# The first layer's mixer shift, scale and gate on TensorE alone, and the first tile turned while their matrices land

## The chip, the cores and the metric

The kernel runs on one core of one Trainium2 chip. The metric is device time in microseconds (us) of one execution; the median of several is compared. Its engines are named as the profile names them: PE (TensorE), DVE (VectorE), ACT (ScalarE), POOL (GpSimd) and SP (SyncE), which issues the DMAs.

## The reference

One inference step of a trunk of two layers, 256 context tokens and 1,024 latent tokens, 1,024 wide. Each sub-layer normalises its rows, applies a scale and a shift that come from a condition vector, runs a mixer or a feed-forward block, and adds the result under a gate from the same condition. What the change touches is the condition's part:

```python
def modulation(cond, w_mod, b_mod):
    m = jax.nn.silu(cond) @ w_mod + b_mod
    return jnp.split(m[:, None, :], 6, axis=-1)

def sublayer_in(x, g, shift, scale):
    return rms_norm(x, g) * (1 + scale) + shift

def sublayer_out(x, y, g, gate):
    return x + gate * rms_norm(y, g)
...
    sh_p, sc_p, gt_p, fsh_p, fsc_p, fgt_p = modulation(c_ctx[None, :], mod_w[l], mod_b[l])
    sh_s, sc_s, gt_s, fsh_s, fsc_s, fgt_s = modulation(c, mod_w[l], mod_b[l])
    hp = sublayer_in(xp, norm_mix_pre[l], sh_p, sc_p)
```

There are two conditions (one for context, one for latents), and `mod_w[l]` is 1,024 x 6,144 in f32: six parts of 1,024 x 1,024. Part 0 is the mixer's shift, part 1 its scale, part 2 its gate.

## The kernel before, in words

Tokens are worked on in ten tiles of 128 rows, in the order 2 to 9, 0, 1 (`ORDER`). A part of `mod_w` is read as eight k tiles of 128 x 1,024 (512 KB each). There are three ways of multiplying a k tile with the two conditions. On DVE, `total[c] = r * cond[k, c] + total[c]` for both c, and at the end four matmuls with `pick` sum the 128 partitions on PE. Or on PE alone: `cond32[:, k]`, the condition padded with zeros to 32 columns, is the stationary operand, and the k tile streams past it in two matmuls of 512 columns. `mod_steps` before mixes both for parts 0 and 1 (`SHARED`: the odd k tiles go to PE, the even ones to DVE, and the pick matmuls add DVE's sums to PE's); the gate (`gate_steps`, part 2) uses DVE and pick, in halves of 512 columns.

**The opening.** Parts 0 and 1 are computed first, from eight buffers `wt`. The result, 64 rows with the two halves at rows 0 and 32, is turned by four small transposes and put into `mods`. Meanwhile the first tile of x is loaded and normalised (`front_rows`), the K/V weights (two units) are loaded and split into a high and a low part (ACT casts, POOL or DVE subtracts), and so are the four Q units.

**The front.** For each tile, a list of events (`weave`, numbers in units of a step; event e of the i-th tile is at i + e) sets by hand the order on PE, DVE, ACT and POOL: `front_load` (x), `front_square` (ACT), `front_rstd` (DVE and POOL), `front_hat` (DVE scales the rows), `front_turn` (PE: eight transposes into an A bank pair), `front_mod` (ACT: eight pieces with `mods`), `front_hi` (DVE: high part into `hh`), `front_lo` (POOL: low part into `hl`), `front_kv` (PE: 24 matmuls of 256 columns), `front_q` (PE: 24 of 512), then head norms, rotary turns (`head_scale`, L489; `head_sum`, L508), the transposed keys and queries and their stores. The gate's generator is advanced twice per tile (0.5 and 0.95). After the front the attention of the latents starts.

SP's order isn't written by hand. It issues one DMA after the other, each waiting for its buffer. Buffers that matter: `wt` 8, `raw` 3 (x tiles, the gate's matrices, the cache), PSUM `bank` B 3, `bank2` A 2.

Of the kernel before, what the change touches and what calls it, by code (L numbers as in the profile page):

```python
# [31 lines left out]
SHARED = (1, 3, 5, 7)  # L32
# [17 lines left out]
def trunk_kernel(ctx: ExitStack, tc: tile.TileContext, A: dict, O: dict):  # L50
# [168 lines left out]
    def mod_steps(l, part, make=None, shared=()):  # L219


        total = [s5([P, D]) for _ in range(2)]

        def load(k):
            r = (make or raw)([P, D])
            SP.dma_start(r, A["mod_w"][l, rows(k), part * D : (part + 1) * D])
            return r

        if shared:
            acc = [bank((64, 512)) for _ in range(2)]  # L230
        nxt = load(0)
        yield
        for k in range(KT):
            r, nxt = nxt, load(k + 1) if k < KT - 1 else None
            if k == 5:
                res = t2([64, 512])
                SP.dma_start(res, A["mod_b"][l, part])
            if k in shared:
                for j in range(2):
                    PE.matmul(acc[j][32 * j : 32 * j + 32, :], cond32[:, k], r[:, 512 * j : 512 * j + 512], start=k == min(shared), stop=False)  # L240
                continue
            for c in range(2):
                if k == 0:
                    DVE.tensor_scalar(total[c], r, cond[:, k, c : c + 1], None, op0=ALU.mult)
                else:
                    DVE.scalar_tensor_tensor(total[c], r, cond[:, k, c : c + 1], total[c], op0=ALU.mult, op1=ALU.add)  # L246
                if c == 0 and (l, part) > (0, 4):
                    yield
            yield
# [5 lines left out]
        if shared:  # L255
            for j in range(2):
                h = slice(32 * j, 32 * j + 32)
                DVE.tensor_tensor(res[h], acc[j][h], res[h], op=ALU.add)
        else:
            DVE.tensor_tensor(res, acc[0][0:64], res, op=ALU.add)  # L260
        yield
        w, what = part // 3, part % 3
        if what == 2:
            for j in range(2):
                SP.dma_start(gate_d[l, w, :, j * 512 : j * 512 + 512], res[32 * j : 32 * j + 2, :])
            return
# [4 lines left out]
        for r in range(2):  # L271
            src = tv[:, :, :, r].rearrange("p b j -> p j b")
            dst = mods[:, l, w, r, 1 - what, :].rearrange("p (j b) -> p j b", b=4)
            if what == 0:
                DVE.tensor_copy(dst, src)
            else:
                gg = gpre[:, l, w, :].rearrange("p (j b) -> p j b", b=4)
                DVE.scalar_tensor_tensor(dst, src, 1.0, gg, op0=ALU.add, op1=ALU.mult)
        yield
# [167 lines left out]
    with tc.manual_schedule(engines=every):  # L447
        finish(mod_steps(0, 0, wt, SHARED))
        front_load(ORDER[0])
        kv_raw = [s5([P, 1024]) for _ in range(2)]  # L450
        for i in range(2):
            SP.dma_start(kv_raw[i], A["wall"][U_KV + i])
        steps = mod_steps(0, 1, wt, SHARED)
        for _ in range(3):
            next(steps)
        front_rows(ORDER[0])
# [4 lines left out]
        finish(steps)  # L461
    early_tiles = ORDER[:1]
# [76 lines left out]
    def front_turn(t):  # L539
        st["tr", t] = tr = bank2((P, KT, P))  # L540
# [109 lines left out]
    def gate_steps(l, w):  # L650

        for j in range(2):
            c = slice(512 * j, 512 * j + 512)
            total = [t2([P, 512]) for _ in range(2)]
            for k in range(KT):
                r = raw([P, 512])
                SP.dma_start(r, A["mod_w"][l, rows(k), (3 * w + 2) * D + 512 * j : (3 * w + 2) * D + 512 * j + 512])
                yield
                for c in range(2):
                    if k == 0:  # L660
                        DVE.tensor_scalar(total[c], r, cond[:, k, c : c + 1], None, op0=ALU.mult)
                    else:
# [5 lines left out]
            yield  # L668
            DVE.tensor_tensor(bias, acc, bias, op=ALU.add)
            SP.dma_start(gate_d[l, w, :, 512 * j : 512 * j + 512], bias[0:2])  # L670
# [3 lines left out]
        (0.06, front_load), (0.5, lambda t: next(front_part, None)), (0.857, front_square), (0.95, front_rstd),  # L674
# [1030 lines left out]
```

## Time and profile before

| | |
|---|---|
| median of 3 runs | 3441.93 us (3436.46 to 3443.43) |
| profiled execution, own time | 3447.16 us |
| its span | 3445.4 us |
| PE busy | 3265.6 us (95%) |
| DVE busy | 2094.1 us (61%) |
| ACT busy | 1266.3 us (37%) |
| POOL busy | 1179.4 us (34%) |
| granted PE clock, mean | 0.982 |

Busy shares are averages over stages with different limits. The granted clock is told as a share: 1.00 is 2.4 GHz, 0.50 is 1.2 GHz, and what lies between is a stretch with some of both.

### The profile page before, as it was taken

The numbers are of one execution on the slowest core, as the hardware profiler recorded it, in microseconds if no ns is written. First come the engines' busy times: TensorE is split into PE (matmuls) and PEld (weight loads), VectorE is DVE, ScalarE is ACT, GpSimd is POOL, SyncE is SP. The second block draws the span as 40 slices with busy tenths as digits, with TensorE's granted clock in tenths as the row PEclk, the third lists the DMA queues.
The fourth block names the chain that finished last, engine by engine and source line by source line (L and its number), as shares of the span: only waits on it lengthen the run. The fifth ranks groups of instructions, "written<-read, shape, count | busy, mean of one in ns | idle before, by whom it ended". The sixth has DMA issues, their size and how long they took to land. (4 is left out here: it accounts for less than half of the span.)

```text
span 3445.4 us, 44445 instructions
## 1 busy us (share of the span) xinstructions
PE 3265.6 (95%) x17258; PEld 2723.2 (79%) x17258; DVE 2094.1 (61%) x3589; ACT 1266.3 (37%) x2529; POOL 1179.4 (34%) x742
## 2 busy tenths in 40 slices
PE   5789999999999999999899999999999999999998
PEld 3667777888878878888778888887778888888886
DVE  7879988546666664344866666666574444344347
ACT  3467863451111111112566666656531111111113
POOL 3556667451111111113644433335221111111134
PEclk8889999999999999999999999999999999999999
DMA  5210023442222221112411111113431111111124
GB/s 208 69 37 14 19 89 114 155 145 87 87 87 88 88 84 40 38 37 86 177 58 45 47 47 45 49 65 97 126 116 45 39 42 43 37 37 37 38 91 165
DMA packets 106211, 260.03 MB, mean 75 GB/s; under 512 B 10240, under 2 KB 45952, under 8 KB 106000
## 3 DMA queue, kind: packets, MB, share of 16 engines
q1 hardware_dynamic: 106000, 257.20, 22.5%
q8 instruction: 135, 2.21, 0.3%
q14 instruction: 76, 0.62, 0.1%
HBM read 221.34 MB, written 35.82 MB: 75 GB/s over the span
## 5 line engine op out<-in xcount | busy, mean ns | idle before, releaser
L1097 DVE TENSOR_TENSOR s<-s,B 128x512 f32<-128x512 f32 x840 | 559.9, 685 | 565.2 <-PE B L192 564.5
L176 POOL TENSOR_TENSOR w<-raw,w 128x1024 fp32r<-128x1024 f32 x163 | 402.6, 2472 | 1408.0 <-ACT w L175 1403.8
L190 PE MATMUL A<-hh,w 128*128 128x512 f32 (+1 forms) x2112 | 755.0, 357 | 3.5 <-DVE s L330 2.2
L192 PE MATMUL A<-hh,w 128*128 128x512 f32 (+1 forms) x2112 | 750.3, 355 | 2.8 <-POOL w L176 2.8
L191 PE MATMUL A<-hl,w 128*128 128x512 f32 (+1 forms) x2112 | 747.7, 354 | 0.0
L190 PEld LDWEIGHTS A<-hh,w 128*128 128x128 f32 x2112 | 397.5, 188 | 69.5 <-issue 5.9
L192 PEld LDWEIGHTS A<-hh,w 128*128 128x128 f32 x2112 | 397.2, 188 | 66.0 <-POOL w L176 4.0
L191 PEld LDWEIGHTS A<-hl,w 128*128 128x128 f32 x2112 | 397.4, 188 | 62.8
L175 ACT CAST w<-raw 128x1024 fp32r<-128x1024 f32 x166 | 174.2, 1049 | 712.7 <-PE B L191 416.1
L190 PE MATMUL B<-w,s 128*128 128x512 f32 x880 | 351.2, 399 | 14.2 <-DVE s L1097 13.5
L192 PE MATMUL B<-w,s 128*128 128x512 f32 x880 | 348.2, 396 | 9.7 <-DVE s L176 8.7
L191 PE MATMUL B<-w,s 128*128 128x512 f32 x880 | 344.0, 391 | 0.0
L1078 ACT ACTIVATE t<-A,c 128x512 f32<-128x512 f32 (+1 forms) x132 | 81.2, 615 | 703.2 <-PE A L192 703.2
L374 PE MATMUL B<-c,s 128*128 128x128 f32 x1344 | 205.8, 279 | 46.8 <-DVE w L390 23.4
L374 PEld LDWEIGHTS B<-c,s 128*128 128x128 f32 x1344 | 155.8, 141 | 90.6 <-DVE w L390 35.7
L190 PE MATMUL C<-hh,w 128*128 128x512 f32 (+1 forms) x576 | 213.0, 370 | 5.2 <-ACT s L1200 1.8
L390 DVE TENSOR_TENSOR t<-B,t 128x512 fp32r<-128x512 f32 (+2 forms) x216 | 127.6, 591 | 142.9 <-ACT t L384 129.6
L190 PEld LDWEIGHTS B<-w,s 128*128 128x128 f32 x880 | 165.3, 188 | 59.2 <-DVE s L1097 27.0
L1079 DVE TENSOR_TENSOR t<-t,A 128x512 f32<-128x512 f32 (+1 forms) x132 | 78.9, 598 | 218.6 <-ACT t L1078 218.6
L192 PEld LDWEIGHTS B<-w,s 128*128 128x128 f32 x880 | 165.4, 188 | 52.5 <-DVE s L176 12.7
L192 PE MATMUL C<-hh,w 128*128 128x512 f32 (+1 forms) x576 | 205.4, 357 | 0.0
L191 PE MATMUL C<-hl,w 128*128 128x512 f32 (+1 forms) x576 | 205.3, 356 | 0.0
(283 smaller groups left out, 6178.9 us busy)
## 6 DMA issues: line engine op xcount, KB each, us to landing
raw<-wall SPq DMA_DIRECT2D x171, 512.0 KB, 3.3
raw<-mod_w SPq DMA_DIRECT2D x72, 512.0 KB, 3.9
x_d<-s SPq DMA_DIRECT2D x30, 512.0 KB, 2.6
w<-wall SPq DMA_DIRECT2D x22, 512.0 KB
raw<-x SPq DMA_DIRECT2D x20, 512.0 KB, 3.9
s<-x_d SPq DMA_DIRECT2D x20, 512.0 KB
s<-wall SPq DMA_DIRECT2D x17, 512.0 KB, 3.4
w<-mod_w SPq DMA_DIRECT2D x16, 512.0 KB, 9.3
```

The lines of the kernel that those rows point to most:

```text
L175: ACT.copy(hi, src)
L176: (eng or DVE).tensor_tensor(lo, src, f32(hi), op=ALU.subtract)
L190: PE.matmul(out, sh, mh, start=i == 0, stop=False)
L191: PE.matmul(out, sh, ml, start=False, stop=False)
L192: PE.matmul(out, sl, mh, start=False, stop=i == n - 1)
L374: PE.transpose(tr[:, at : at + P], self.p[a][:, col : col + P], ident)
L390: DVE.tensor_tensor(tl[:, 0:n], tr[:, 0:n], f32(th[:, 0:n]), op=ALU.subtract)
L1078: ACT.activation(s, acc[:, 0, 0:n], AF.Silu, bias=zerob)
L1079: DVE.tensor_tensor(s, s, acc[:, 1, 0:n], op=ALU.mult)
L1097: DVE.tensor_tensor(yt, yt, part, op=ALU.add)
```

## The change

Parts 0 and 1 come from PE alone. The matrices of both are loaded in one row (the first eight into the eight `wt` buffers, each of part 1 as soon as the matmuls of the same k of part 0 are through), and each is multiplied by two matmuls when it is there; the two halves go to different 32-row groups of PSUM. x of the first tile is loaded ahead of everything, normalised at once and turned on PE between the third and fourth matrix of part 1. The gate of the first layer's mixer is multiplied on PE too, one k tile per step with the full 1,024 columns, into 32 rows of an A bank pair that it holds through the front. x of the second tile is loaded ahead of the Q units. `mod_steps` loses its shared form; for the other parts it stays as it was.

```diff
@@ -216,54 +215,13 @@
-    def mod_steps(l, part, make=None, shared=()):
...
-        if shared:
-            acc = [bank((64, 512)) for _ in range(2)]
...
-            if k in shared:
-                for j in range(2):
-                    PE.matmul(acc[j][32 * j : 32 * j + 32, :], cond32[:, k], r[:, 512 * j : 512 * j + 512], start=k == min(shared), stop=False)
-                continue
-            for c in range(2):
-                if k == 0:
-                    DVE.tensor_scalar(total[c], r, cond[:, k, c : c + 1], None, op0=ALU.mult)
-                else:
-                    DVE.scalar_tensor_tensor(total[c], r, cond[:, k, c : c + 1], total[c], op0=ALU.mult, op1=ALU.add)
-                if c == 0 and (l, part) > (0, 4):
-                    yield
...
-        if not shared:
-            acc = [bank_c()] * 2
-        for j in range(2):
-            for c in range(2):
-                PE.matmul(acc[j][32 * j : 32 * j + 32, :], pick[:, c, :], total[c][:, 512 * j : 512 * j + 512], start=c == 0 and not shared, stop=c == 1)
...
+    def mod_load(l, part, k, make):
+        r = make([P, D])
+        SP.dma_start(r, A["mod_w"][l, rows(k), part * D : (part + 1) * D])
+        return r
+
+    def mod_put(l, w, what, res):
+
         tr = bank_c((P, 4, 64))
         for b in range(4):
             PE.transpose(tr[:, b, :], res[:, b * P : (b + 1) * P], ident[0:64, 0:64])
...
+    def first_mods():
+
+        parts = [(part, k) for part in range(2) for k in range(KT)]
+        there = {item: mod_load(0, *item, wt) for item in parts[:KT]}
+        acc, res = {}, {}
+        for part, k in parts:
+            if k == 0:
+                acc[part] = [bank((64, 512)) for _ in range(2)]
+                res[part] = t2([64, 512])
+                SP.dma_start(res[part], A["mod_b"][0, part])
+            r = there.pop((part, k))
+            for j in range(2):
+                PE.matmul(acc[part][j][32 * j : 32 * j + 32, :], cond32[:, k], r[:, 512 * j : 512 * j + 512], start=k == 0, stop=k == KT - 1)
+            if part == 0:
+                there[1, k] = mod_load(0, 1, k, wt)
+            yield
+            if k == KT - 1:
+                for j in range(2):
+                    h = slice(32 * j, 32 * j + 32)
+                    DVE.tensor_tensor(res[part][h], acc[part][j][h], res[part][h], op=ALU.add)
+                mod_put(0, 0, part, res[part])
+                yield
...
@@ -436,7 +452,7 @@
     st = {}
 
     def front_load(t):
-        if t not in early_tiles:
+        if t not in early_tiles and ("x", t) not in st:
             st["x", t] = x_load(A["x"][rows(t), :])
 
     def front_rows(t):
@@ -445,20 +461,27 @@
 
     early_tiles = ()
     with tc.manual_schedule(engines=every):
-        finish(mod_steps(0, 0, wt, SHARED))
         front_load(ORDER[0])
+        steps = first_mods()
+        for _ in range(2):
+            next(steps)
+        front_rows(ORDER[0])
+        for _ in range(10):
+            next(steps)
         kv_raw = [s5([P, 1024]) for _ in range(2)]
         for i in range(2):
             SP.dma_start(kv_raw[i], A["wall"][U_KV + i])
-        steps = mod_steps(0, 1, wt, SHARED)
-        for _ in range(3):
+        st["tr", ORDER[0]] = tr = bank2((P, KT, P))
+        for k in range(KT):
+            PE.transpose(tr[:, k, :], st["xh", ORDER[0]][:, k, :], ident)
+        for _ in range(5):
             next(steps)
-        front_rows(ORDER[0])
         kv_units = []
         for i in range(2):
             kv_units.append((s5([P, 1024], F32R), s5([P, 1024], F32R)))
             split(*kv_units[i], kv_raw[i], POOL)
         finish(steps)
+    front_load(ORDER[1])
     early_tiles = ORDER[:1]
     q_raw = [s5([P, 1024]) for _ in range(4)]
     for i in range(4):
@@ -537,6 +560,8 @@
             DVE.tensor_scalar(xh, st.pop(("x", t)), st.pop(("rs", t)), None, op0=ALU.mult)
 
     def front_turn(t):
+        if t in early_tiles:
+            return
         st["tr", t] = tr = bank2((P, KT, P))
         for k in range(KT):
             PE.transpose(tr[:, k, :], st["xh", t][:, k, :], ident)
@@ -649,29 +674,26 @@
     qpairs, qparts = [(2, 3), (4, 5), (6, 7), (8, 9), (0, 1)], None
     def gate_steps(l, w):
 
+        part = 3 * w + 2
+        r = mod_load(l, part, 0, raw)
+        yield
+        acc = bank2()
+        for k in range(KT):
+            for j in range(2):
+                PE.matmul(acc[0:32, 512 * j : 512 * j + 512], cond32[:, k], r[:, 512 * j : 512 * j + 512], start=k == 0, stop=k == KT - 1)
+            if k < KT - 1:
+                r = mod_load(l, part, k + 1, raw)
+                yield
+        bias = raw([32, 2, 512])
         for j in range(2):
-            c = slice(512 * j, 512 * j + 512)
-            total = [t2([P, 512]) for _ in range(2)]
-            for k in range(KT):
-                r = raw([P, 512])
-                SP.dma_start(r, A["mod_w"][l, rows(k), (3 * w + 2) * D + 512 * j : (3 * w + 2) * D + 512 * j + 512])
-                yield
-                for c in range(2):
-                    if k == 0:
-                        DVE.tensor_scalar(total[c], r, cond[:, k, c : c + 1], None, op0=ALU.mult)
-                    else:
-                        DVE.scalar_tensor_tensor(total[c], r, cond[:, k, c : c + 1], total[c], op0=ALU.mult, op1=ALU.add)
-            bias, acc = raw([32, 512]), bank((32, 512))
-            SP.dma_start(bias, A["mod_b"][l, 3 * w + 2, 32 * j : 32 * j + 32])
-            for c in range(2):
-                PE.matmul(acc, pick[:, c, :], total[c], start=c == 0, stop=c == 1)
-            yield
-            DVE.tensor_tensor(bias, acc, bias, op=ALU.add)
-            SP.dma_start(gate_d[l, w, :, 512 * j : 512 * j + 512], bias[0:2])
+            SP.dma_start(bias[:, j], A["mod_b"][l, part, 32 * j : 32 * j + 32])
+        yield
+        DVE.tensor_tensor(bias, acc[0:32].rearrange("p (j n) -> p j n", j=2), bias, op=ALU.add)
+        SP.dma_start(gate_d[l, w].rearrange("r (j n) -> r j n", j=2), bias[0:2])
 
     front_part = gate_steps(0, 0)
     rest = weave(at_each(enumerate(ORDER), [
-        (0.06, front_load), (0.5, lambda t: next(front_part, None)), (0.857, front_square), (0.95, front_rstd),
+        (0.06, front_load), (0.857, front_square), (0.95, front_rstd),
         (0.95, lambda t: next(front_part, None)), (1.303, front_hat), (1.66, front_turn), (1.875, lambda t: front_mod(t, 0)),
```

What this does to the engines' orders is shown at three places. In SP's order the loads of the opening were: eight matrices (with a bias), x, two K/V units, eight matrices (with a bias), four Q units. Now they are x, eight matrices, a bias, eight matrices, a bias, two K/V units, x of the second tile, the gate's first matrix, four Q units.

The first place is ACT in the opening, from the K/V casts to the square of the third tile; s_29 (now) and s_40 (before) are the first tile's rows, s_72 and s_80 the second's, A its turned form. Before:

```order
L175 CAST s_41_180<-s_26_149 128x1024
L175 CAST s_43_184<-s_27_150 128x1024
L175 CAST w_242<-s_51_222 128x1024
L175 CAST w_246<-s_52_223 128x1024
L175 CAST w_250<-s_53_224 128x1024
L175 CAST w_254<-s_54_225 128x1024
L528 ACTIVATE s_80_288,sm_289<-raw_268,c_70 128x1024
L547 ACTIVATE s_40_178<-A_279,c_74 128x128 x8
L528 ACTIVATE s_89_350,sm_351<-raw_303,c_70 128x1024
```

Now:

```order
L174 CAST s_43_201<-s_40_178 128x1024
L174 CAST s_45_205<-s_41_179 128x1024
L174 CAST w_241<-s_49_221 128x1024
L174 CAST w_245<-s_50_222 128x1024
L551 ACTIVATE s_72_266,sm_267<-raw_219,c_70 128x1024
L174 CAST w_249<-s_51_223 128x1024
L572 ACTIVATE s_29_133<-A_182,c_74 128x128
L174 CAST w_253<-s_52_224 128x1024
L572 ACTIVATE s_29_133<-A_182,c_74 128x128 x7
L551 ACTIVATE s_81_325,sm_326<-raw_282,c_70 128x1024
```

The square of the second tile has moved between the Q casts, and the first piece of the modulation of the first tile ahead of the last cast, the other seven behind it.

The second place is DVE from the second lo part of the Q weights to the first tile's cast into hh and the next tile's; t_72 and t_73 are the gate's sums for the two conditions, raw_262 and the like its matrices. Before:

```order
L176 TENSOR_TENSOR w_255<-s_54_225,w_254 128x1024
L472 TENSOR_SCALAR s_55_230<-s_55_230 128x64
L661 TENSOR_SCALAR t_72_260<-raw_262,c_77 128x512
L661 TENSOR_SCALAR t_73_261<-raw_262,c_77 128x512
L663 SCALAR_TENSOR_TENSOR t_72_260<-raw_266,c_77,t_72_260 128x512
L663 SCALAR_TENSOR_TENSOR t_73_261<-raw_266,c_77,t_73_261 128x512
L203 TENSOR_SCALAR sm_295<-sm_289 128x1
L663 SCALAR_TENSOR_TENSOR t_72_260<-raw_272,c_77,t_72_260 128x512
L663 SCALAR_TENSOR_TENSOR t_73_261<-raw_272,c_77,t_73_261 128x512
L550 CAST hh_72<-s_40_178 128x8x128
L537 TENSOR_SCALAR s_80_288<-raw_268,sm_296 128x1024
L663 SCALAR_TENSOR_TENSOR t_72_260<-raw_301,c_77,t_72_260 128x512
```

Now:

```order
L175 TENSOR_TENSOR w_254<-s_52_224,w_253 128x1024
L495 TENSOR_SCALAR s_53_229<-s_53_229 128x64
L575 CAST hh_72<-s_29_133 128x8x128
L560 TENSOR_SCALAR s_72_266<-raw_219,sm_274 128x1024
L202 TENSOR_SCALAR sm_332<-sm_326 128x1
L502 TENSOR_REDUCE sm_343<-t_87_342 128x2
L202 TENSOR_SCALAR sm_346<-sm_343 128x2
L575 CAST hh_72<-s_72_266 128x8x128
L560 TENSOR_SCALAR s_81_325<-raw_282,sm_333 128x1024
```

The gate's multiply-adds are gone from between the tiles' own operations.

The third place is PE in the first step, at the end of one tile's KV matmuls (B_325 and B_300) and the start of its Q matmuls (B_381 and B_356). Before:

```order
L190 MATMUL B_325<-s_43_184,hh_72 128x256
L191 MATMUL B_325<-s_44_185,hh_72 128x256
L192 MATMUL B_325<-s_43_184,hl_73 128x256
L190 MATMUL B_381<-w_242,hh_72 128x512
L191 MATMUL B_381<-w_243,hh_72 128x512
L192 MATMUL B_381<-w_242,hl_73 128x512
```

Now, with the gate's second matrix raw_280 between the two:

```order
L189 MATMUL B_300<-s_45_205,hh_72 128x256
L190 MATMUL B_300<-s_46_206,hh_72 128x256
L191 MATMUL B_300<-s_45_205,hl_73 128x256
L683 MATMUL A_277<-raw_280,t_9_80 32x512 x2
L189 MATMUL B_356<-w_241,hh_72 128x512
L190 MATMUL B_356<-w_242,hh_72 128x512
L191 MATMUL B_356<-w_241,hl_73 128x512
```

Each of the eight steps now has two such matmuls with 32 rows of output.

## Rows read from the trace of the kernel before

**Rows 1.** The page's head.

```profile
span 3445.4 us, 44445 instructions
```

**Rows 2.** Windows by front_hi: length, busy by engine, PEclk, DMA share, GB/s.

```profile
53.41:63.46 10.05, 8.65 (x41) 8.18 (x42) 5.15 (x10) 4.37 (x12) 3.89 (x3) 0.63 0.35 111
63.46:75.55 12.09, 12.09 (x70) 10.40 (x69) 10.85 (x21) 6.18 (x19) 7.98 (x9) 1.00 0.45 150
121.25:137.85 16.60, 12.59 (x62) 11.24 (x61) 13.24 (x28) 6.71 (x20) 7.69 (x7) 0.79 0.26 79
63.46:153.21 89.75, 70.45 (x359) 58.68 (x358) 74.77 (x152) 38.27 (x109) 47.37 (x40) 0.87 0.28 87
153.21:166.88 13.67, 11.64 (x67) 9.88 (x68) 11.09 (x24) 6.78 (x20) 7.27 (x6) 1.00 0.08 23
166.88:178.01 11.13, 11.08 (x67) 9.50 (x67) 8.48 (x24) 5.48 (x16) 7.59 (x5) 1.00 0.09 25
178.01:200.24 22.23, 15.80 (x82) 13.57 (x80) 12.98 (x35) 7.22 (x22) 11.69 (x8) 0.86 0.21 60
```

**Rows 3.** Timeline, DVE in the opening: start, duration, instruction, idle time before it.

```profile
5.67 1.41 DVE L244 TENSOR_SCALAR s<-w,c 128x1024 f32<-128x1024 f32 x2 [5.67 <-DMA w<-mod_w]
...
30.16 11.15 DVE L246 SCALAR_TENSOR_TENSOR s<-w,c,s 128x1024 f32<-128x1024 f32 x4
...
52.08 1.41 DVE L663 SCALAR_TENSOR_TENSOR t<-raw,c,t 128x512 f32<-128x512 f32 x2 [1.45 <-DMA raw<-mod_w]
```

**Rows 4.** Timeline, ACT and SP in the opening.

```profile
32.25 1.04 ACT L175 CAST w<-s 128x1024 fp32r<-128x1024 f32 x1 [11.58 <-DMA s<-wall]
...
47.26 2.90 ACT L547 ACTIVATE s<-A,c 128x128 f32<-128x128 f32 x8 [3.72 <-DVE c L278]
...
54.82 0.33 SPq L323 DMA_DIRECT2D raw<-x  x1
...
59.09 1.15 ACT L528 ACTIVATE s<-raw,c 128x1024 f32<-128x1024 f32 x1 [8.93 <-DMA raw<-x]
```

**Rows 5.** The window from the first landing to the first Q unit.

```profile
5.67:32.25 26.58, 15.02 (x46) 3.74 (x48) 19.15 (x19) 3.34 (x5) 5.42 (x3) 0.90 1.03 385
```

**Rows 6.** Timeline, PE in the front.

```profile
113.88 0.55 PE L190 MATMUL B<-s,hh 128*128 128x256 f32 x1 [4.02 <-ACT s L478]
...
151.24 1.91 PE L667 MATMUL B<-t,c 128*32 128x512 f32 x4
```

**Rows 7.** Timeline, DVE ahead of that KV matmul.

```profile
109.31 1.40 DVE L663 SCALAR_TENSOR_TENSOR t<-raw,c,t 128x512 f32<-128x512 f32 x2
...
113.45 0.29 DVE L489 TENSOR_TENSOR t<-B,sm 128x128 f32<-128x128 f32 x1
```

**Rows 8.** DVE's costliest group from 47 to 170 us: busy, mean ns, idle before.

```profile
L663 DVE SCALAR_TENSOR_TENSOR t<-raw,c,t 128x512 f32<-128x512 f32 x28 | 24.0, 894 | 3.8 <-DMA raw<-mod_w 3.8
```

**Rows 9.** Windows: PE alone over one step without waits; all engines after a wait.

```profile
171.12:181.19 10.07, 10.02 (x63) 1.00 0.11 30
...
113.90:120.00 6.10, 6.10 (x29) 5.96 (x30) 4.63 (x12) 3.46 (x9) 2.95 (x3) 0.59 0.38 110
```

**Rows 10.** Timeline, PE in the opening.

```profile
15.81 1.92 PE L240 MATMUL B<-w,t 128*32 128x512 f32 x4 [1.67 <-DMA w<-mod_w]
...
22.50 1.05 PE L240 MATMUL B<-w,t 128*32 128x512 f32 x4
...
30.30 1.97 PE L542 MATMUL A<-c,s 128*128 128x128 f32 x8 [4.48 <-DVE s L293]
...
41.37 3.63 PE L254 MATMUL B<-s,c 128*32 128x512 f32 x6 [1.37 <-DVE s L246]
```

**Rows 11.** Timeline, POOL behind the first front_hi.

```profile
54.18 2.80 POOL L553 TENSOR_TENSOR hl<-s,hh 128x1024 fp32r<-128x1024 f32 x1 [2.91 <-DVE hh L550]
```

More of the change, by code (lines that the diff above doesn't have):

```diff
@@ L31 @@
 AFTER = 0
-SHARED = (1, 3, 5, 7)
 NEG = -1e30
@@ L216, in filler @@
         return fill
-    def mod_steps(l, part, make=None, shared=()):
[L222 to L227, printed above, removed]
-        if shared:
-            acc = [bank((64, 512)) for _ in range(2)]
-        nxt = load(0)
-        yield
-        for k in range(KT):
[L234 to L237, printed above, removed]
-            if k in shared:
-                for j in range(2):
-                    PE.matmul(acc[j][32 * j : 32 * j + 32, :], cond32[:, k], r[:, 512 * j : 512 * j + 512], start=k == min(shared), stop=False)
-                continue
-            for c in range(2):
-                if k == 0:
-                    DVE.tensor_scalar(total[c], r, cond[:, k, c : c + 1], None, op0=ALU.mult)
-                else:
-                    DVE.scalar_tensor_tensor(total[c], r, cond[:, k, c : c + 1], total[c], op0=ALU.mult, op1=ALU.add)
-                if c == 0 and (l, part) > (0, 4):
-                    yield
-            yield
-        if not shared:
-            acc = [bank_c()] * 2
-        for j in range(2):
-            for c in range(2):
-                PE.matmul(acc[j][32 * j : 32 * j + 32, :], pick[:, c, :], total[c][:, 512 * j : 512 * j + 512], start=c == 0 and not shared, stop=c == 1)
[L255 to L258, printed above, removed]
-        else:
[L260 to L266, printed above, removed]
+    def mod_load(l, part, k, make):
[3 more added lines that the diff above has]
+    def mod_put(l, w, what, res):
         tr = bank_c((P, 4, 64))
@@ new lines, in mod_steps, with load @@
+    def mod_steps(l, part):
+        total = [s5([P, D]) for _ in range(2)]
+        def load(k):
+            return mod_load(l, part, k, raw)
+        nxt = load(0)
+        yield
+        for k in range(KT):
+            r, nxt = nxt, load(k + 1) if k < KT - 1 else None
+            if k == 5:
+                res = t2([64, 512])
+                SP.dma_start(res, A["mod_b"][l, part])
+            for c in range(2):
+                if k == 0:
+                    DVE.tensor_scalar(total[c], r, cond[:, k, c : c + 1], None, op0=ALU.mult)
+                else:
+                    DVE.scalar_tensor_tensor(total[c], r, cond[:, k, c : c + 1], total[c], op0=ALU.mult, op1=ALU.add)
+                if c == 0 and (l, part) > (0, 4):
+                    yield
+            yield
+        acc = bank_c()
+        for j in range(2):
+            for c in range(2):
+                PE.matmul(acc[32 * j : 32 * j + 32, :], pick[:, c, :], total[c][:, 512 * j : 512 * j + 512], start=c == 0, stop=c == 1)
+        DVE.tensor_tensor(res, acc[0:64], res, op=ALU.add)
+        yield
+        w, what = part // 3, part % 3
+        if what == 2:
+            for j in range(2):
+                SP.dma_start(gate_d[l, w, :, j * 512 : j * 512 + 512], res[32 * j : 32 * j + 2, :])
+            return
+        mod_put(l, w, what, res)
@@ L539, in front_turn @@
     def front_turn(t):
+        if t in early_tiles:
+            return
         st["tr", t] = tr = bank2((P, KT, P))
@@ L650, in gate_steps @@
     def gate_steps(l, w):
[L652 to L670 removed]
+        part = 3 * w + 2
+        r = mod_load(l, part, 0, raw)
+        yield
+        acc = bank2()
+        for k in range(KT):
+            for j in range(2):
+                PE.matmul(acc[0:32, 512 * j : 512 * j + 512], cond32[:, k], r[:, 512 * j : 512 * j + 512], start=k == 0, stop=k == KT - 1)
+            if k < KT - 1:
+                r = mod_load(l, part, k + 1, raw)
+                yield
+        bias = raw([32, 2, 512])
+        for j in range(2):
+            SP.dma_start(bias[:, j], A["mod_b"][l, part, 32 * j : 32 * j + 32])
+        yield
+        DVE.tensor_tensor(bias, acc[0:32].rearrange("p (j n) -> p j n", j=2), bias, op=ALU.add)
+        SP.dma_start(gate_d[l, w].rearrange("r (j n) -> r j n", j=2), bias[0:2])
     front_part = gate_steps(0, 0)
     rest = weave(at_each(enumerate(ORDER), [
[L674 removed]
+        (0.06, front_load), (0.857, front_square), (0.95, front_rstd),
         (0.95, lambda t: next(front_part, None)), (1.303, front_hat), (1.66, front_turn), (1.875, lambda t: front_mod(t, 0)),
```

## The prediction

> **What bounds the kernel now.** The page gives the span, 3445.4 us [rows 1]; the profiled execution took 3447.16 us, 1.76 us more, and lies 5.2 us above the median of the runs shown, 3441.93. The difference worked out below is taken off that median. The page's 40 slices show PE nearly full everywhere but at the front, so I read the front by stages: the stretches between successive starts of front_hi (L550), one per tile of tokens [rows 2]. Three things are to be seen there. The first tile's front_hi, without which no projection starts, comes at 53.41 us. From then on a step takes 10.05, then 12.09 to 16.60, and 11.13 us in the last one, which has no gate work. And in the six steps from 63.46 to 153.21 PE is busy for 70.45 of 89.75 us and is granted 0.87 of its clock, while DVE is busy for 74.77.
>
> Next I asked what ends the opening. The chain is: DVE's L246 sums, four of them 11.15 us long from 30.16 [rows 3]; PE's pick matmuls, which end at 45.00 [rows 10]; the modulation on ACT from 47.26 for 2.90 us [rows 4]; and then 3.25 us until front_hi at 53.41, because DVE stands first at a gate sum that waits for its matrix (the 1.45 us wait at 52.08 [rows 3]). The loads aren't that chain: the first lands at 5.67 and the twentieth (a Q unit) at 32.25 [rows 3, 4], with the DMA engines full (share 1.03) at 385 GB/s [rows 5].
>
> Last, what ends the steps of the front. PE's first KV matmul waits 4.02 us and starts at 113.88 [rows 6], right behind DVE's L489 (113.45 + 0.29 us), which is the last reader of the PSUM bank that it needs [rows 7]. DVE comes to L489 late since the gate's multiply-adds stand ahead of it, such as the pair at 109.31. After the wait PE runs 6.1 us at granted 0.59 [rows 9]. So DVE's order sets the step, and PE pays twice.
>
> **The change, part by part.** *Opening.* All DVE sums and pick matmuls of parts 0 and 1 go. Each matrix costs two matmuls into different column groups, four records: 1.05 us at the fast clock, 1.92 at the slow one [rows 10]. One load takes 26.58 us / 19.5 = 1.363 us (twenty loads from the first landing to the last, less the first, and two biases of a quarter load each). At 1.05 us PE keeps up with the landings; part 1's last matrix is the 17th load and lands at 5.67 + 16.5 x 1.363 = 28.2. With 1.05 and, as before, 2.26 us from the last matmul to ACT's start (45.00 to 47.26), mods are there at about 31.5.
>
> But ACT isn't free then: its new order puts the Q casts ahead, the last of them between the first and the other seven pieces of the modulation. That cast waits for the 25th load: 5.67 + 24.5 x 1.363 = 39.1 us. With the cast (1.04) and seven eighths of 2.90 us [rows 4], front_hi comes at 42.7. On DVE no gate sum stands in front of it now, so the 3.25 us go. Before it was 53.41: **10.7 us earlier**. The second tile's load still waits for front_hat and lands too late for ACT's square as before (8.93 us wait, [rows 4]), so I leave the first step at 10.05. front_lo on POOL (2.80 us, [rows 11]) follows front_hi in both orders.
>
> The Trainium skill, DMA: Bandwidth & Descriptors, Specifications, gives some 358 GB/s of HBM per core. The trace had 385, so the measurement decides. By an estimate with the page's figure the 25th load would land some 2.5 us later and the sum would lose as much.
>
> *Front.* DVE loses 28 multiply-adds, 24.0 us busy and 3.8 us of waits for their matrices [rows 8]. PE loses four pick matmuls and gains sixteen, two per step in eight steps, of which the first lies in the opening and the second in the step that I leave as it is. They write the same 32 rows, as L667 does, whose two matmuls took 1.91 us at granted 1.00 [rows 6], so they don't overlap; from below 1.05, if they did. Without a wait PE needs 10.07 us from one turn to the next step's query turn [rows 9]. With the gate: 11.98. DVE's loop without gate work is at most the 11.13 us of the last step [rows 2]. PE becomes the bound of the step. I take 12.3 us, 0.3 above the sum for joints; bounds are 11.2 (matmuls overlap) and 13.0 (one more microsecond of waiting on DVE's L489). The six steps took 89.75 us [rows 2]; at 12.3 they take 73.8: **16.0 us less**. The next one, 13.67, held the last pick matmuls and a PE wait, and has no gate matmul now: 11.13, **2.5 us less**. The last two stretches stay.
>
> *Waits added.* The gate's accumulator holds one of two A buffers, so a turn must wait for the modulation of the tile before. That costs nothing while KV of that tile stands right behind the turn and needs front_hi and front_lo after the same modulation (front_lo alone is 2.80 us, [rows 11]); without this cover a turn (1.97 us at the slow clock, [rows 10]) would be added to each step, at most. An x load now waits for a gate matmul to free its raw buffer, with the query store ahead of it in SP's queue. ACT wants that x only after the Q matmuls behind the gate (24 of 512 columns where KV has 24 of 256, so more than half of the 10.07 us); a load needs 4.3 us (issued at 54.82, taken at 59.09, [rows 4]). It is hidden by about a microsecond. Turning the first tile early costs 1.97 us of PE [rows 10] while it waits for matrices.
>
> **Sum.** 10.7 + 16.0 + 2.5 = 29 us: 3447 to 3418 for the profiled execution, and **3413 us** from the median. With the bounds (start 6 to 12, six steps 11.75 to 22.5, the last 2.5) it is 20 to 37, so 3405 to 3422; the start's 6 is the first rival's, its 12 an estimate for loads that lose 4 per cent less than the 26.58 us show.
>
> **Rivals.** *PE stays slow in the opening.* For it: the four-record groups took 1.92 us until 15.81 and 1.05 only at 22.50, after a stretch without gaps [rows 10]. Then sixteen matrices cost 30.7 us of PE, more than their landing, which takes 22: 7.0 (the second load) + 30.7 + 2.0 (the turn) + 2.3 between the parts = 42.0, then 2.26 to ACT and 2.90 there: front_hi at 47.2, a gain of 6.2 for 10.7. Total 24.5, 3417. Against it: at 1.92 the engine has no gaps left, and the faster rows came after just such a stretch. Chance 0.14. [...]
>
> *The gate matmuls keep the front at a mixed clock.* If PE still waits for DVE's bank, its clock falls with the wait as at 113.9 to 120 [rows 9] and the gate pair costs twice 1.91: 10.07 + 3.82 + 0.6 for a KV at the lower clock, steps of 14.5, six of them 87 us. 10.7 + 2.75 + 2.5 = 16, 3426. Against it: DVE's loop is shorter than PE's sum. Chance 0.12.
>
> *The time is given back behind the front.* 22.23 us lie between the last front_hi and the first scores, with PE idle for 6.4 of them [rows 2]; if loads or ACT's tail held this end at its old time, the gain would vanish: 3438 to 3442. Nothing read there waits for more than the front's own work. Chance 0.08.
>
> *Slower: x late behind the gate.* Place: SP's queue and the three raw buffers. If the chain gate, x load, square, scale and turn doesn't fit into a step, ACT stands at the square with the modulation behind it, and PE at the turn. The opening's 10.7 and the 2.5 of the step without gate work must first be lost: six steps at (89.75 + 13.2) / 6 = 17.2 us, so a wait of over 5 us in each decides; at 6 us, 18.0 each, it is 3447. For it: ACT's 8.93 us wait for x shows how an x load that waits for a buffer stops ACT [rows 4]. Against it: this wait has the Q matmuls for cover. Chance 0.08.
>
> **How the numbers follow.** My forecast has 0.58, with its own range of 3405 to 3422. The first rival lies in it; the range goes on to 3431 for the second and to 3403 for bounds that meet at the quick end, and leaves out the last two, 0.16. A change of 0.2%, 7 us, is about what a measurement can tell here. Faster by more: 0.58 + 0.14 + 0.12, 0.84 with nothing for the rest; the third rival gives 0.08 for the same, the fourth 0.08 for slower.
>
> **What would show it.** Right: front_hi first at 41 to 45 us, behind the last Q cast; steps near 12.3 with PE busy all through and granted 1.00; the 4 us waits before KV gone; gate pairs at 1.91 us; the last front_hi near 149 us for 178. Wrong: four-record groups of 1.92 us past 25 us, casts waiting past 42, ACT waiting at the square for x in every step, or PE waiting for DVE's L489 as before. It would also be wrong if the stretch from the last front_hi to the first scores grows by what the front saves.

## The result, and the profile after

The changed kernel took 3422.54 us (median of 4 runs, 3420.81 to 3426.11), the kernel before 3440.4 us on the same chip (4 runs). The ratio is 0.995, with a 95% interval of 0.9933 to 0.9967: faster by 18 us where 29 were forecast. That is inside the whole range of the prediction (3403 to 3431), and half a microsecond above the forecast's own (3405 to 3422). The profiled execution took 3424.07 us. In a second comparison of the same two kernels on another chip the ratio was 0.9924 (below), so part of the shortfall is scatter between chips and executions.

The first fence shows the page's head, and then windows of after between starts of front_hi (L575 now), with the columns of [rows 2]. The row from 53.50 to 122.68 holds the same six steps as the one from 63.46 to 153.21 there; the row below it has one step more.

```profile
span 3422.3 us, 44448 instructions
...
43.61:53.50 9.89, 8.40 (x41) 6.54 (x42) 1.96 (x7) 4.32 (x12) 4.10 (x3) 0.76 0.18 57
53.50:63.97 10.47, 10.47 (x58) 7.91 (x57) 6.97 (x17) 6.44 (x19) 7.75 (x8) 1.00 0.45 149
63.97:75.62 11.65, 11.65 (x63) 8.85 (x62) 9.20 (x21) 5.28 (x14) 8.13 (x6) 1.00 0.27 92
75.62:87.07 11.45, 11.45 (x65) 8.72 (x64) 8.65 (x26) 6.70 (x19) 8.12 (x6) 1.00 0.34 114
98.93:110.81 11.88, 11.88 (x66) 9.11 (x66) 8.65 (x25) 6.69 (x19) 8.14 (x6) 1.00 0.33 110
53.50:122.68 69.18, 69.18 (x379) 52.80 (x377) 50.76 (x128) 38.52 (x109) 48.40 (x38) 1.00 0.33 109
53.50:134.56 81.06, 81.06 (x448) 63.19 (x447) 60.54 (x152) 45.21 (x128) 56.54 (x44) 1.00 0.31 103
134.56:145.68 11.12, 10.42 (x65) 8.98 (x64) 8.48 (x24) 5.46 (x16) 7.61 (x5) 1.00 0.09 26
145.68:166.90 21.22, 14.22 (x81) 11.95 (x80) 13.53 (x35) 7.17 (x22) 11.67 (x8) 0.94 0.21 62
```

The first front_hi comes at 43.61 us for 53.41. In the six steps from 53.50 on PE is busy for every one of 69.18 us, at granted 1.00, where it was busy for 70.45 of 89.75 at 0.87 [rows 2]: PE has become the bound of the front. The seventh step is the same (81.06 us in all). The last front_hi comes at 145.68 for 178.01, **32.3 us** earlier, and the stretch behind it has not grown (21.22 for 22.23). The front alone thus saved more than the 29 forecast. PE's waits from 53 to 146 us are one row (waited for: total, times, longest), where one wait alone took 4.02 in [rows 6]:

```profile
PE B L189 <- ACT s L501: 0.7, 1, 0.7
```

The timeline of after's opening (start, duration, instruction, idle time before it), PE, then ACT, then DVE:

```profile
7.01 6.44 PE L250 MATMUL B<-w,t 128*32 128x512 f32 x20 [7.01 <-DMA w<-mod_w]
13.67 1.05 PE L250 MATMUL B<-w,t 128*32 128x512 f32 x4 [0.22 <-DMA w<-mod_w]
...
28.22 1.05 PE L250 MATMUL B<-w,t 128*32 128x512 f32 x4 [0.90 <-DMA w<-mod_w]
...
37.12 1.14 ACT L551 ACTIVATE s<-raw,c 128x1024 f32<-128x1024 f32 x1
...
39.56 1.03 ACT L174 CAST w<-s 128x1024 fp32r<-128x1024 f32 x1
40.49 2.54 ACT L572 ACTIVATE s<-A,c 128x128 f32<-128x128 f32 x7
...
31.24 0.24 DVE L236 SCALAR_TENSOR_TENSOR c<-C,c 128x8 f32<-128x8 f32 x2 [0.55 <-PE C L227]
...
40.62 2.97 DVE L175 TENSOR_TENSOR w<-s,w 128x1024 fp32r<-128x1024 f32 x1 [1.05 <-ACT w L174]
...
43.61 0.68 DVE L575 CAST hh<-s 128x1024 fp32r<-128x1024 f32 x1
```

The modulation values are there at 31.5 us (L236), ACT is through with the seven pieces at 43.03, and DVE comes to front_hi when its own subtraction for a Q unit ends, at 43.59.

So the question is where 32 us became 18 to 26.

### The profile page after: what moved, and what is told of

It is laid out like the page before. It is cut to its first block, busy times and chain, and to the rows that moved or that the text cites. A ratio compares the mean times of both kernels' runs of the same rounds, so it can differ in the third digit from the quotient of the medians.

```text
span 3422.3 us, 44448 instructions
## 1 busy us (share of the span) xinstructions
PE 3269.2 (96%) x17298; PEld 2718.1 (79%) x17298; DVE 2039.9 (60%) x3540; ACT 1265.1 (37%) x2529; POOL 1180.7 (34%) x742
```

## The experiments

The kernels were timed in four sets. All kernels of one set shared a chip with the kernel before, whose median there was 3446.02, 3446.44, 3446.66 and 3450.22 us. "Saved" is one less the ratio, times that median. The profile of an execution is single; the times are not, except where said.

Three theories were set against each other. **A, chance:** single executions differ because PE's clock falls in some gaps and not in others, and the work behind the front is the same. **B, given back:** what is behind the front takes longer whenever the front ends earlier. **P, placement**, which came up after the first set: the change moved the on-chip buffers.

### Both kernels again, and each half of the change alone

No edit for the first two.

> The kernel before once more, unchanged, for a second profile and for the spread. The two traces at hand have the first scores 33.3 us earlier after the change, but the medians differ by 17.9 us only. Theory A (chance): the stage behind the front has the same work; single executions differ by some us since PE's clock falls in some gaps and not in others, and the first profile of before is one of the slow ones. Then this trace has front_hi first at 53.4 and its first scores within 3 us of 200.2, and differs from the first one by 4 to 8 us behind that. Theory B (given back): the back takes longer whenever the front ends earlier; then this trace is like the first one behind the front within 2 us. Ratio 1.000 by both.

> The changed kernel once more, unchanged, in five rounds. Both theories: first scores at 166.9 within 2 us. Theory A: the back differs from the first trace of this kernel by 2 to 8 us, and the ratio lies at 0.992 to 0.996. Theory B: the back is as in the first trace within 2 us, 0.995.

The opening alone: the changed opening, with `gate_steps` and its two events per step as before.

```diff
 (after.py)
-        (0.06, front_load), (0.857, front_square), ...
+        (0.06, front_load), (0.5, lambda t: next(front_part, None)), (0.857, front_square), ...
     def gate_steps(l, w):      # the body of before.py: totals on DVE, 512 columns at a time
```

> The opening of the change alone: parts 0 and 1 on TensorE, the first tile turned early; the gate stays on DVE in halves. By the prediction's sum: front_hi first at 43 to 47 us (the gate sums stand ahead of it again, so up to 3.25 later than the 43.6 of the whole change), steps of 14 to 17 us as before, first scores 7 to 10 us earlier than the 200.2 of before. Theory A: time 7 to 10 us less, ratio 0.997 to 0.998. Theory B: some half of that, 0.999.

The gate alone: the kernel before, with `gate_steps` and the event list of the changed one.

> The gate on TensorE alone; the opening stays as before. By the prediction's sum: front_hi first at about 50.2 (53.4 less the 3.25 us behind DVE's gate sum), steps of 11.5 to 12.3 us, first scores 22 to 25 us earlier than the 200.2 of before. Theory A: time 22 to 25 us less, ratio about 0.993. Theory B: some half of that, 0.9965.

Measured: before 3445.28 us (10 runs, ratio 1.0, 0.9991 to 1.0009), after 3421.32 (5 runs, **0.9924**, 0.9912 to 0.9937), the opening alone 3447.12 (11 runs, **1.0002**, 0.9993 to 1.0011), the gate alone 3422.46 (5 runs, **0.9926**, 0.9914 to 0.9938). The gate gives all of the time and the opening none, though with the opening alone the first scores (L704 in before) came 10.5 us earlier (188.8 for 199.3). Theory B in its plain form falls with the gate alone: its scores came 26.2 us earlier, and 25.5 us were saved.

The difference lies in the products behind the front. The next fence has rows of the groups by line from 2600 to 3400 us, in the second layer's SwiGLU: the three matmuls of an output product (high x high, high x low, low x high), count, busy, mean ns, idle; the kernel before again, then the changed one again.

```profile
L190 PE MATMUL B<-w,s 128*128 128x512 f32 x380 | 150.6, 396 | 1.2 <-DVE s L1097 1.2
L191 PE MATMUL B<-w,s 128*128 128x512 f32 x380 | 148.1, 390 | 0.0
L192 PE MATMUL B<-w,s 128*128 128x512 f32 x380 | 149.9, 394 | 0.2 <-DVE s L176 0.2
```

```profile
L189 PE MATMUL B<-w,s 128*128 128x512 f32 x384 | 152.0, 396 | 1.9 <-DVE s L1119 1.9
L190 PE MATMUL B<-w,s 128*128 128x512 f32 x384 | 151.6, 395 | 0.0
L191 PE MATMUL B<-w,s 128*128 128x512 f32 x384 | 151.1, 394 | 1.2 <-DVE s L175 1.2
```

The second of the three takes 395 ns for 390. Both kernels that have the new opening show it, the gate alone does not (390). The code of this product is untouched. What the opening did change is in the compiled programs, which are not among the kept traces: the buffers of a kind get their addresses when the first of them is used. Before, that was s5, wt, raw, sm; now x is loaded first, then the matrices go to wt, and s5 comes last. The s5 buffers, which hold the stationary operand here, went from byte 94,848 of each partition to 140,288, that is from 128 above a multiple of 512 to a multiple of 512; wt, the moving operand, stayed at 128 above one (181,888, then 107,136). The distances agree with the sizes in the kernel: 17 s5 buffers of 5,120 bytes lie between 94,848 and 181,888, and three raw buffers of 4,096 between 94,848 and 107,136.

### The buffers put elsewhere

Three kernels touch one column of a tile of each kind, in a chosen order, and compute the same. The edit is this line at the head of the schedule, for after with the placement of before:

```diff
     with tc.manual_schedule(engines=every):
+        for tile in (s5([P, 1]), wt([P, 1])):
+            POOL.memset(tile, 0.0)
```

> The changed kernel, but one column of a tile of s5 and one of wt are set before anything else, so that the on-chip buffers of s5, wt, raw and sm lie at the addresses that they have in the kernel before. No computation is changed. Theory P (placement: the change moved the buffers, and the output product of the SwiGLU units, L189 to L191, reads from addresses that cost 5 ns more per matmul): the mean of its second matmul (output from w and s) falls from 395 to 390 ns, the stretch from the first silu of the SwiGLU units to the last falls from 2672 to 2674 us to 2667 us, and the time from 3421 to 3415 us. Theory A (chance, PE's clock in single gaps): nothing systematic, 395 ns and 3421 us. Theory B (what the front gives is taken back behind it, whatever is placed where): 3421 us.

For before with the placement of after:

```diff
+        for tile in (raw([P, 1]), wt([P, 1]), sm(1), s5([P, 1])):
+            POOL.memset(tile, 0.0)
```

> The kernel before, but one column each of a raw, a wt, an sm and an s5 tile is set first, in this order, so that these buffers lie at the addresses that they have in the changed kernel. Nothing else is changed. Theory P: the second matmul of the output product goes from 390 to 395 ns, the silu stretch from 2667 to 2672 to 2676 us, and the time from 3446 to 3451 to 3455 us, with the front as it was. Theories A and B: 390 ns, 2667 us and 3446 us, since the front ends when it did.

For after with s5 alone moved, by 128 bytes:

```diff
+        for tile in (raw([P, 1]), wt([P, 1]), sm(1), sm(8), s5([P, 1])):
+            POOL.memset(tile, 0.0)
```

> The changed kernel with its own order of buffers, but one more sm tile of 8 values is set ahead of the first s5 tile, which moves all s5 buffers up by 128 bytes (from a multiple of 512 bytes to 128 above one, as in the kernel before) and leaves wt and raw where they are. Theory P has two forms. P1 (the 512 bytes that 128 stationary values take in each partition want the offset that they have in the kernel before): 390 ns, a silu stretch of 2667 us and 3415 us, as with the whole placement of before. P2 (it is where wt lies against s5 and the products' other operands): 395 ns, 2672 to 2674 us and 3421 us. Theories A and B: as P2.

Measured: after with the placement of before 3418.73 us (5 runs, 0.9913, 0.9899 to 0.9926); before with the placement of after 3451.44 us (12 runs, **1.0017**, 1.0006 to 1.0027); after with s5 128 bytes up 3417.82 us (6 runs, **0.9915**, 0.9902 to 0.9928). The matmul answers to each: 390, 395 and 390 ns. The fence has it for before with after's placement, and then for after with the 128 bytes, same stretch and columns:

```profile
L191 PE MATMUL B<-w,s 128*128 128x512 f32 x381 | 150.4, 395 | 0.0
```

```profile
L190 PE MATMUL B<-w,s 128*128 128x512 f32 x384 | 149.8, 390 | 0.0
```

128 bytes decide, with raw and wt left where they were: P1 and not P2, as they were put here (the other offsets below change this). The kernel before gets 5 us slower by the move of its buffers alone. For the changed kernel the two intervals with the better offset overlap that of the changed kernel in the first set, so the gain in time there (0.9924 to about 0.9914) is by itself not beyond the scatter.

The whole stretch of the SwiGLU units, from silu to silu, was no clean measure, against what the expectations said: after with the 128 bytes had 390 ns and a stretch of 2676 us, since this execution lost time in PE's gaps. Taken apart, it is one. Each trace has 133 stretches between successive silus, in the same order (the starts of ACT's silu in the timelines); two are long and hold other work. Compared one by one with after in the placement of before, the five traces with s5 at 0 or 256 and wt at 128 have the same medians: 53 ns more in the 40 stretches near 16.6 us, 72 to 73 ns more in the 46 of 17 to 25 us, and 5 to 7 ns less in the 45 under 14 us. In the traces with s5 at 128 all three medians lie within 6 ns of nothing. By an estimate from these rows (count times median) the offset costs 5.2 us, in both traces of the changed kernel as in the others. The gaps are Theory A's, and real. The windows show two neighbouring stretches of the first layer's SwiGLU, from silu to silu, in the kernel before again and then in the changed one again:

```profile
978.31:994.89 16.58, 16.58 (x75) 13.56 (x74) 15.62 (x18) 2.36 (x3) 2.84 (x1) 1.00 0.39 121
994.89:1004.83 9.94, 8.15 (x59) 7.36 (x58) 7.33 (x7) 3.32 (x4) 2.68 (x1) 1.00 0.25 74
```

```profile
947.71:964.35 16.64, 16.64 (x75) 13.57 (x74) 15.64 (x18) 2.37 (x3) 3.17 (x1) 1.00 0.40 122
964.35:975.49 11.14, 9.15 (x57) 8.19 (x56) 7.23 (x6) 3.31 (x4) 2.88 (x1) 0.85 0.30 92
```

The first pair of rows differs by the offset: 16.58 and 16.64 us of gapless PE work. The second differs by chance: PE waits in either for DVE's subtraction (1.79 and 1.99 us), but in the one execution its clock is granted at 1.00 throughout and in the other at 0.85, and the stretch is 1.2 us longer. Such falls struck other executions with either offset: 0.86 in after with s5 up (967.49 to 978.50 us), 0.85 in the opening alone (901.39 to 913.13).

### The opening alone with the offset restored

```diff
 (the opening alone)
+        for tile in (raw([P, 1]), wt([P, 1]), sm(1), sm(8), s5([P, 1])):
+            POOL.memset(tile, 0.0)
```

> The opening change alone (the gate on VectorE in halves, as before), with one more sm tile of 8 values ahead of the first s5 tile, which moves the s5 buffers 128 bytes up, off the multiples of 512 bytes. The opening change alone without that move gave nothing (3447.1 against 3446.0 us), though its first scores came 10.5 us earlier. Theory P1 (the s5 buffers at multiples of 512 bytes cost some 5 us in the products behind the front): 390 ns in the second matmul of the output product in place of 395, and a time of 5 us less than the opening change alone: 3442 us where the kernel before takes 3446. Theory A2 (what the opening gives is lost to PE's clock in gaps that come with the new opening, wherever the buffers lie): 3447 us still.

Measured 3442.54 us (12 runs, **0.9983**, 0.9974 to 0.9991), with 390 ns. The interval lies wholly under that of the opening alone (1.0002, 0.9993 to 1.0011): some 6 us from the offset, and the opening saves time after all. A2 falls.

### Other offsets

After with s5 256 bytes above a multiple of 512 (`sm(8), sm(2)` in the line above), and after with s5 at the multiple and wt moved 384 bytes up, to a multiple too (`raw, sm(1), wt, s5`).

> The changed kernel with two more sm tiles ahead of the first s5 tile: the s5 buffers at 256 bytes above a multiple of 512. Only the mean of the second matmul of the output product is asked for. P1 in the form that only multiples of 512 are dear: 390 ns. In the form that only the offset of 128 that s5 then has in common with wt is cheap: 395 ns.

> The changed kernel with its s5 buffers where they are (at multiples of 512 bytes) and the wt buffers 384 bytes higher, at multiples of 512 too, by touching the first sm tile ahead of the first wt tile. The s5 buffers 128 bytes above a multiple gave 390 ns in the second matmul of the output product, at 0 and 256 bytes they gave 395, and wt stood at 128 in all of these. Two forms are left. P3 (s5 and wt want the same offset within 512 bytes): 390 ns and 3417 us. P4 (s5 wants the offset 128 wherever wt lies): 395 ns and 3421 us or more, if the products with wt as their stationary operand grow as well.

The first was a single run, 3429.99 us, with 395 ns: not only multiples of 512 are dear. The second took 3420.0 us (5 runs, 0.9914, 0.99 to 0.9928). Here are its rows, then those of after again, from 2600 to 3400 us: the output product and the product ahead of it, which has wt as its stationary operand and hl as the moving one of its second matmul (hh and hl lie 192 bytes above a multiple of 512).

```profile
L190 PE MATMUL A<-hl,w 128*128 128x512 f32 x608 | 239.9, 395 | 0.0
L189 PE MATMUL B<-w,s 128*128 128x512 f32 x384 | 151.3, 394 | 1.9 <-DVE s L1121 1.9
```

```profile
L190 PE MATMUL A<-hl,w 128*128 128x512 f32 x608 | 237.2, 390 | 0.0
```

P4 falls, and P3 holds only in part: with s5 and wt at a common offset of 0 the output product's matmuls took 394, 393 and 391 ns (1178 together, for 1185 in after), but the product with hl and wt grew from 390 to 395. In the attention's output product (610 to 720 us), where one operand lies in wt and the other in s5, the second matmul took 394 ns in after, 389 with s5 at 128 and 389 with both at 0. In all of these products it fits that what counts is how the two operands stand to each other within 512 bytes: equal or 64 apart was cheap, 128 or 192 apart was dear. Why, these runs don't tell. For the whole kernel, both kinds at 0 is no clear gain: its SwiGLU stretches have medians of 133 ns more (near 16.6 us), 156 more (17 to 25) and 189 less (under 14) than after in the placement of before, by the same estimate 4.0 us where s5 alone at 0 costs 5.2, and its time can't be told from that of after (0.9914 and 0.9924, with intervals that overlap).

### The gate's products in two groups

The gate's two matmuls per matrix write the same 32 output rows. This kernel gives each half its own, as the opening does, and has the placement of before:

```diff
-                PE.matmul(acc[0:32, 512 * j : 512 * j + 512], cond32[:, k], ...
+                PE.matmul(acc[32 * j : 32 * j + 32, 512 * j : 512 * j + 512], cond32[:, k], ...
...
-        DVE.tensor_tensor(bias, acc[0:32].rearrange("p (j n) -> p j n", j=2), bias, op=ALU.add)
+        for j in range(2):
+            h = slice(32 * j, 32 * j + 32)
+            DVE.tensor_tensor(bias[h], acc[h, 512 * j : 512 * j + 512], bias[h], op=ALU.add)
...
```

> The changed kernel with the buffers placed as in the kernel before, and the two halves of the gate's products in two groups of 32 output rows, as the opening has them, in place of one. In the opening a pair in two groups starts 1.05 us apart and in the front a pair in one group takes 1.91 us. If PE bounds a front step (10.07 us of its own work and 1.91 us of the gate: 11.98; measured 11.45 to 11.88), the seven steps with gate products fall to 11.1 us, the last front_hi comes 5 us earlier, and the time is 5 us below that of the changed kernel with the same placement: 3410 us by theory P, 3416 us without it. If the pair costs 1.9 us in either form when it stands between other matmuls, the steps stay at 11.9 us and the time at 3415 or 3421 us.

Measured 3411.96 us (5 runs, **0.9901**, 0.9887 to 0.9915). The second kernel has the groups, and s5 128 bytes up:

> The changed kernel with the s5 buffers 128 bytes higher and the gate's products in two groups of 32 output rows. The kernel with the groups and the placement of before measured steps of 11.1 us and 3412 us, but its dummy tiles also changed the order of the opening's loads, so that its first front_hi came at 45.9 us and not 43.1 to 43.6. Sum: first front_hi at 43.1, seven steps of 11.1 us in place of 11.8, so the last front_hi at 141 us, 4 to 5 us before that of the run with the 128 bytes alone (145.99), and 3413 us against its 3418. If groups and offset don't add up (Theory B: the back takes what the front gives), 3417 us.

Measured 3412.11 us (4 runs, **0.9899**, 0.9887 to 0.9912), with the first front_hi at 43.33 and the last at 141.33 us. Its pair and two of its steps (timeline, then windows by front_hi):

```profile
94.29 1.05 PE L685 MATMUL A<-raw,t 128*32 128x512 f32 x4
...
85.52:96.65 11.13, 11.13 (x67) 8.92 (x66) 8.55 (x25) 6.71 (x19) 8.10 (x6) 1.00 0.42 122
96.65:107.79 11.14, 11.14 (x67) 8.84 (x66) 8.55 (x25) 6.72 (x19) 8.10 (x6) 1.00 0.38 119
```

In after the pair stood in the timeline so:

```profile
108.89 1.90 PE L683 MATMUL A<-raw,t 128*32 128x512 f32 x4
```

1.05 us for 1.90, and a step of 11.13 where after had 11.88. This version beats both kernels: 35 us under the one before, and its slowest run, 3415.34, is under the fastest of the changed kernel, 3419.93. Against after with s5 128 bytes up (3417.82) the two intervals still overlap. The extra tiles of the placement of before also turned the order of the opening's loads (first front_hi at 45.9 us), which is why the offset alone was the better way to the same time.

### What the front gains and what is saved

Lead: how much earlier the first scores started than in the kernel before again (199.3 us).

| kernel | s5 above 512 | lead, us | saved, us |
|---|---|---|---|
| opening alone | 0 | 10.5 | -0.7 |
| changed kernel, first comparison | 0 | 32.4 | 17.2 |
| changed kernel again | 0 | 33.0 | 26.2 |
| before, placement of after | 0 | -0.6 | -5.9 |
| opening alone, s5 up | 128 | 6.1 | 5.9 |
| gate alone | 128 | 26.2 | 25.5 |
| after, placement of before | 128 | 28.4 | 30.0 |
| after, s5 up | 128 | 31.1 | 29.3 |
| groups, placement of before | 128 | 33.9 | 34.1 |
| groups, s5 up | 128 | 35.7 | 34.8 |
| after, s5 as it is, wt moved | 0, wt too | 31.1 | 29.7 |

After at 256, a single run, is left out. With the offset of before the lead is kept within 2 us in every kernel; with s5 alone at 0, 5 to 15 us of it are lost, of which the offset's price explains 5. The savings carry an uncertainty of 3 to 6 us and the leads are of single executions (the opening alone had 6.1 in one and 10.5 in the other), so the rest stays open for the first two rows, and the 2 us of the last row don't speak against the 4 us that its stretches lose.

## Why the prediction was right, and where it was off

**The opening: 10.7 forecast, 9.8 measured.** The steps held nearly one by one. The last matrix of part 1, the 17th load, was taken at 28.22 (forecast 28.2); PE kept up at 1.05 us per matrix from 13.67 on; the modulation values were there at 31.5; the last Q cast stood between the first piece of modulation and the other seven. But this cast didn't wait for the 25th load, as the prediction had it: it stood behind the second tile's square on ACT (37.12), whose x is now there in time, and ran at 39.56 without a wait. It ended within half a microsecond of the forecast, by another chain. Of the 0.9 us that are missing, 0.3 are ACT's, which is through at 43.03 for 42.7, and 0.6 are DVE's subtraction for that Q unit, which ends at 43.59 and wasn't counted.

Two readings behind this part don't hold in the trace of the kernel before. The fence has its windows of two four-record groups (length, PE busy, PEclk, DMA share, GB/s), and then ACT's square of the second tile from its timeline:

```profile
15.81:17.73 1.92, 1.92 (x6) 1.00 1.03 412
22.50:23.55 1.05, 1.05 (x6) 1.00 1.02 410
...
42.30 1.15 ACT L528 ACTIVATE s<-raw,c 128x1024 f32<-128x1024 f32 x1
```

The group of 1.92 us stands at granted 1.00 just as the one of 1.05 does, so the rows don't show that a slow clock made it slow; what did is open. And the 8.93 us wait was for the third tile's x: the second tile's square ran at 42.30 without a wait. The first step, left at 10.05 for that wait, took 9.89.

**The six steps: 16.0 forecast, 20.6 measured** (69.18 us from 53.50 to 122.68). That PE becomes the bound was right, and so was its sum, 11.98: the last three of the six are 11.86 to 11.88, with gate pairs of 1.90 us. The first three were shorter, 10.47, 11.65 and 11.45, with 58, 63 and 65 matmul records for 66; the forecast took all six alike. The 0.3 for joints was not there, since PE never waits, and neither was the price of DVE's L489. **The step behind: 2.5 forecast, 1.8 measured:** PE was still behind (its first wait comes at 140.31), so the stretch took 11.88 and not 11.13.

**Behind the front: nothing forecast, some 5 us lost.** This is the step that failed: the sum ends at the first scores and puts all that lies behind them at nothing, as if untouched code took its old time. The front's 32.3 us outdid the forecast, and the offset of s5, which no row of before could show, took 5 of them (5.2 by the SwiGLU stretches of both traces of the changed kernel; before with this placement alone: 1.0017; the opening alone with and without: some 6 us). The rest of the difference to 18 us is no term of the sum. The changed kernel took 3422.5 and 3421.3 us in the two comparisons, but the kernel before took 3440.4 in the first (four runs) and 3446.0 to 3450.2 in the four sets behind it. Most of the step from 18 to 26 saved thus lies in that first time of the kernel before; why it was lower there is open.

**The number.** 3422.54 us is 9.5 above the forecast of 3413, and the 18 us saved are under the forecast's own least of 20. The measured time lies inside the whole range because this was widened to 3431 for a mixed clock in the front, and that did not come. That it fell inside is luck; that the change is faster, and that PE bounds the front, is not. Inside the front errors cancelled too: 0.9 us too much for the opening and 0.7 for the step behind, 4.6 too little for the six steps.

**The rivals.** PE slow in the opening: no; the first five matrices took 6.44 us, 1.29 each, and from 13.67 on each took 1.05 (this rival's sum, 6.2 + 16.0 + 2.5, is 24.7 and not 24.5). A mixed clock in the front: no, granted 1.00 in all of 81.06 us. Given back behind the front: for the opening alone it came true in its size, but not by its mechanism. Neither loads nor ACT's tail held the end of its front: the stretch from the last front_hi (168.37) to the first scores (188.84) took 20.5 us for 22.23. The products behind it grew, by some 5 of the 11 us, and the rest is open. x late behind the gate: no, PE waits for nothing there.

## What to carry to other kernels

An edit can move the buffers of the whole program, and then code that it doesn't touch changes its time; compare the means of untouched matmuls between the two traces, by form, before reading a small difference as the edit's own. Where an accumulation has few output rows, two halves in different 32-row groups cost 1.05 us here, in one group 1.90, and on an engine that bounds the stage most of this came back (0.75 of 0.85 us in a step). And a gain in an early stage was kept to the end, within the 2 us that can be told here, wherever the later work was the same.

## What the runs showed of the hardware that was not expected

A matmul of 128x512 in the split products has a mean of 390 or of 395 ns by where its two operands lie within 512 bytes of a partition, in a stream where PE has no gaps; moving one kind of buffer by 128 bytes switches it, at some 5 us per execution of this kernel. With wt at 128 above a multiple, s5 at 128 was cheap and at 0 and 256 dear. In a gap of nearly the same length (1.79 and 1.99 us), one execution kept the granted clock at 1.00 and the other fell to 0.85 over 11.14 us.
